# Key lookups of one pair of tiles moved to VectorE, and the norms of each pair done for both tiles together

## The chip, the cores and the metric

The kernel runs on one core of a Trainium2 chip. Its engines are TensorE (PE, matrix products), VectorE (DVE), ScalarE (ACT), GpSimd (POOL) and SyncE (SP), which only issues transfers here. The metric is the device time of one execution in microseconds.

## The reference

The kernel computes one layer for 1024 tokens of width 1024, in float32. A first sub-layer mixes tokens with a convolution module and a recurrence (RWKV-7), joins both in one output projection, and a second sub-layer retrieves single-neuron experts by product keys (PEER). Each sub-layer ends in a residual sum and a LayerNorm. What the change touches is the seam between the two:

```python
y1 = jnp.concatenate([y_conv, y_rw], axis=-1) @ w_out
x = layer_norm(ALPHA * x + gate1[:, None, :] * y1, ln1_g, ln1_b)

h2 = adaln(x, shift2, scale2)                       # a second LayerNorm
q = (h2 @ peer_wq).reshape(bsz, seq, PEER_HEADS, PEER_QDIM)
s1, s2 = ...                                        # scores against 128 keys per head and half
v1, i1 = lax.top_k(s1, PEER_TOPK)                   # 16 best of each half
v2, i2 = lax.top_k(s2, PEER_TOPK)
cand = (v1[..., :, None] + v2[..., None, :])        # 16 x 16 sums
sc, ci = lax.top_k(cand.reshape(...), PEER_TOPK)    # 16 best of these
experts = (jnp.take_along_axis(i1, ci // PEER_TOPK, axis=-1) * PEER_NKEYS
           + jnp.take_along_axis(i2, ci % PEER_TOPK, axis=-1))
gates = jax.nn.softmax(sc, axis=-1)
```

The two `take_along_axis` are the key lookups: for each of the 16 chosen candidates of a head, which key of the first half and which of the second it came from. Then each token's 128 experts give `gelu(h2 . u) * gate`, and the sum of their rows of `peer_v` is y2.

## The kernel before, in words

The 1024 tokens are eight tiles of 128; tiles go in pairs (0 and 1, 2 and 3, 4 and 5, 6 and 7). The kernel has three stages. In the first, the input projections of both halves are made. In the second, a loop over 16 chunks of 64 tokens carries the recurrence, and other work is strewn between its small products. In the third, the dense stage (lines 1222 to 1296), the activations of tiles 0 to 4 against all 16384 experts are computed on TensorE and weighted with a gate matrix, while tiles 5, 6 and 7 fetch the rows of their own experts from memory (`gather`, line 1137).

Three generators make the work between the stages, one pair at a time. `front` (line 776) makes the output projection, eight groups of products against `w_out`, brings the result back to rows by transposes (line 813), adds it to x (814), normalises, applies g1 and b1 (817 on VectorE, 818 on GpSimd), stores x1 (819), and normalises again for the second sub-layer; for a tile that will gather it also stores the modulated rows h2 (824 to 826). `query` (831) brings the normalised tiles to channels (`to_channels`, 217), makes sixteen projections against `wq` (line 858), whose weights come by `load_split` (167, three buffers), then the scores (866) and the 16 best of each (`best16`, 768). For tiles 6 and 7 the scores are only stored, and chosen from in the dense stage (`choose_late`, 880). For the others `choose` (892) finds the candidates and does the lookups: for each half of the key and each group of four heads, it compares a ramp with the chosen position (943, VectorE), multiplies with the indices (946, on the engine `E` that the caller names), and sums over sixteen places, on GpSimd in three halving sums and a last one (952, 954), on VectorE in one reduction (949). The caller names GpSimd for tiles 0 to 5 (878), and VectorE for tiles 6 and 7 (890).

When `choose` of a tile of the dense stage has ended, its `gate_matrix` (970) turns the chosen keys into the 128 x 128 gate of each token, four tokens at a time: comparisons on VectorE (1003, 1007), a multiply on GpSimd (1009), ScalarE for every fourth token (1012, 1013), a product on TensorE (1015), a copy into a stage buffer (1016) and one store of 2 MB for each 32 tokens (1023). The gate matrix of tile 4 is the last; its last block goes to the dense stage in SBUF (`gfirst`).

The last pair's `front`, then `query` of tiles 4 and 5, then `query` of tiles 6 and 7 stand in one list, `side`, and are stepped one after the other (line 1077); the lookups stand in the list `slow`, one step for every second step of `side`; the gates in the list `gates`, one step for every twelfth, at raised priority. The program order so written is the priority by which a planner, with its own estimate of durations, sets the order on each engine. On the chip each engine then runs its instructions in that order. Buffers are handed out by pools: `mm` has three PSUM banks, `page` 31 pages of SBUF, and `page2`, which the last pair's `front` and the lookups of tiles 4 and 5 use, 12 pages of 512 values.

Of the kernel before, what the change touches and what calls it, by code (L numbers as in the profile page):

```python
# [21 lines left out]
S = 1024  # L22
# [4 lines left out]
NH = 8  # L27
# [13 lines left out]
PB = 256  # L41
# [17 lines left out]
GPRI = 500  # L59
P2C = 1  # L60
NP2 = 12
PIN = 3
STEPS = 4, 3
RATES = 1.0, 1.0
# [19 lines left out]
def layer_kernel(ctx, tc, x, cols, c_row, cond_w, w_in, w2a2, g2, w_out, ln_rows, wq, keys, peer_u, peer_ut, peer_v, peer_vt, out):  # L84
    nc = tc.nc
    V, A, G, T = nc.vector, nc.scalar, nc.gpsimd, nc.tensor
# [10 lines left out]
    def col(n, i=None):  # L97
        a, b = COFF[n]
        return colt[:, a:b] if i is None else colt[:, a + i:a + i + 1]
# [53 lines left out]
    def mm(w=512):  # L153
        return psum.tile([128, 512], F32, tag="mm", name="mm")[:, :w]
# [4 lines left out]
    def page(name, dt=F32, w=512):  # L159
        return pgp.tile([128, max(w, 512)], dt, tag="pg", name=name)[:, :w]  # L160
# [49 lines left out]
    def normalize(dst, src):  # L210
        m, r = stats(src)
        b = small.tile([128, 1], F32, name="nbias")
        V.scalar_tensor_tensor(b, m, -1.0, r, op0=OP.mult, op1=OP.mult)
        for d_, s_ in zip(dst, src):
            A.activation(d_, s_, AF.Identity, bias=b, scale=r)
# [34 lines left out]
    def cond_some(js, pool=fe):  # L250

        for j in js:
            w = pool.tile([128, D], F32, tag="wraw", name="cw", bufs=WRAW if pool is fe else CBUF)
            ld(w, cond_w[j])
            with behind(0) if PIN & 2 else nullcontext():
                V.scalar_tensor_tensor(w, w, 1.0, silc, op0=OP.mult, op1=OP.mult, accum_out=mod[:, j:j + 1])
# [16 lines left out]
    def load_x(t, pg_):  # L273
        parts = [pg_("xt") for _ in range(2)]
        for i in range(2):
            ld(parts[i], x[128 * t:128 * t + 128, 512 * i:512 * i + 512])
        return parts
# [172 lines left out]
    slow, gates, gb, conv_left, psg, selbank = [], [], [], [], [], [None]  # L450
    ready = {}

    def behind(h):
        return tc.issue_after(ready[h].ins) if h in ready else nullcontext()
    PE_TAPS = 13

    def conv(h):
        acc = []
        for ct in range(4):
# [4 lines left out]
            acc.append(a)  # L464
            with behind(0) if PIN & 1 else nullcontext():
                V.tensor_scalar(a, win(0), wk(0), col("conv_b", ct), op0=OP.mult, op1=OP.add)
# [92 lines left out]
    for l in range(6):  # L559
# [6 lines left out]
        nm = rc.tile([128, 64], F32, name=f"offm{l}", bufs=1)  # L566
# [31 lines left out]
    kept, ys, late, normed, page2, st3, blocks = {}, {}, [], {}, [], [], [0]  # L598
# [164 lines left out]
    def duo(name, dt=F32, pg_=page):  # L763

        ps = [pg_(name, dt).rearrange("p (a t) -> p a t", a=2) for _ in range(KD // 2)]
        return ps, [ps[k // 2][:, k % 2, :] for k in range(KD)]
# [9 lines left out]
    def front(t0, pg_):  # L776

        n, nt, tile0 = PB, PB // 128, t0 // 128
        fetch = [tile0 + t in GT for t in range(nt)]
        hp, hi = duo("ychi", F32R, pg_)  # L780
        lp, lo = duo("yclo", F32R, pg_)
        for i in range(KD // 2):
            f = pg_("ycf").rearrange("p (a t) -> p a t", a=2)
            if i < 2:
                c = t0 % HALF
                ld(f, conv_d[t0 // HALF][2 * i:2 * i + 2, :, c:c + n].rearrange("g p t -> p g t"))
            else:
                for t in range(nt):
                    ld(f[:, :, 128 * t:128 * t + 128],
                       rwkv_d[tile0 + t][2 * i - 4:2 * i - 2].rearrange("g p t -> p g t"))  # L790
            A.activation(hp[i], f, AF.Copy)
            G.tensor_sub(lp[i], f, hp[i].bitcast(F32))
        yield
        y1 = duo("y1", F32, pg_)[1]
        for j in range(KD):
            w = load_split(w_out, j)
            pt = mm(n)
            yield from proj(w, (hi, lo), pt)
            A.activation(y1[j], pt, AF.Copy, scale=mod[:, 16 + j:17 + j])
        rows = {}  # L800
        for nm, src in (("g1", ln_rows[0]), ("b1", ln_rows[1])) + (
                (("sh2", mod_d[3]), ("sc2", mod_d[4])) if any(fetch) else ()):
            rows[nm] = [pg_("row_" + nm) for _ in range(2)]
            s_ = src.rearrange("a b -> (a b)") if len(src.shape) == 2 else src
            for i in range(2):
                ld(rows[nm][i], s_[512 * i:512 * i + 512][None, :].to_broadcast([128, 512]))
        xn = []
        for t in range(nt):
            xt = load_x(tile0 + t, pg_)
            for i in range(2):  # L810
                pt = mm()
                for k in range(4):
                    T.transpose(pt[:, 128 * k:128 * k + 128], y1[4 * i + k][:, 128 * t:128 * t + 128], ident)
                V.scalar_tensor_tensor(xt[i], xt[i], ALPHA, pt, op0=OP.mult, op1=OP.add)
            normalize(xt, xt)
            for i in range(2):
                V.tensor_mul(xt[i], xt[i], rows["g1"][i])
                G.tensor_add(xt[i], xt[i], rows["b1"][i])
                ld(x1_d[tile0 + t][:, 512 * i:512 * i + 512], xt[i])
            xs = [pg_("xn2") for _ in range(2)]  # L820
            normalize(xs, xt)
            if fetch[t]:
                for i in range(2):
                    V.scalar_tensor_tensor(xt[i], rows["sc2"][i], 1.0, xs[i], op0=OP.add, op1=OP.mult)
                    G.tensor_add(xt[i], xt[i], rows["sh2"][i])
                    ld(h2_d[tile0 + t][:, 512 * i:512 * i + 512], xt[i])
            xn.append(xs)
            yield
        normed[t0] = xn

    def query(t0):

        n, nt, tile0 = PB, PB // 128, t0 // 128
        fetch = [tile0 + t in GT for t in range(nt)]
        xn = normed.pop(t0)
        hi, lo = duo("h2hi", F32R)[1], duo("h2lo", F32R)[1]

        def keep(k, h, l):
            for w, f in enumerate((h, l)):
                for t in range(nt):  # L840
                    if not fetch[t]:
                        d = 128 * DT.index(tile0 + t)
                        ld(h2t_d[w, k, :, d:d + 128], f[:, 128 * t:128 * t + 128].bitcast(F32))

        to_channels(xn, lambda k: mod[:, 24 + k:25 + k], lambda k: modp[:, k, 1:2], hi, lo, keep)
        yield
        vi = [page("vi").rearrange("p (q h a r) -> p q h a r", q=2, h=NH, a=2) for t in range(nt)
              if tile0 + t not in score_d]
        val = [t[:, 0] for t in vi]
        idx = [t[:, 1].bitcast(U32) for t in vi]  # L850
        for g in range(4):
            kt = pgp.tile([128, 4, 128], F32, tag="pg", name="keys")
            ld(kt, keys[:, 4 * g:4 * g + 4, :])
            qt = []
            for m in range(4):
                w = load_split(wq, 4 * g + m)
                pt = mm(n)
                yield from proj(w, (hi, lo), pt)
                if m % 2 == 0:
                    qp = page("qt").rearrange("p (a t) -> p a t", a=2)  # L860
                A.activation(qp[:, m % 2, :], pt, AF.Copy)
                qt.append(qp[:, m % 2, :])
            for t in range(nt):
                ps = mm()
                for m in range(4):
                    T.matmul(ps[:, 128 * m:128 * m + 128], qt[m][:, 128 * t:128 * t + 128], kt[:, m, :],
                             start=True, stop=True)
                s = page("s12")
                A.activation(s, ps, AF.Copy)
                if tile0 + t in score_d:  # L870
                    ld(score_d[tile0 + t][g], s)
                    yield
                    continue
                for m in range(4):
                    best16(val[t][:, 2 * g + m // 2, m % 2], idx[t][:, 2 * g + m // 2, m % 2], s[:, 128 * m:128 * m + 128])
                    yield
        for t in range(len(vi)):
            slow.append(choose(tile0 + t, val[t], idx[t], 0, NH, 4, lambda nm, d, w, p=page2[0] if t0 == S - 2 * PB and P2C else page: p(nm, d, w), G))

    def choose_late(tt, lt):  # L880

# [191 lines left out]
    st3.append(pg2x.enter_context(tc.tile_pool(name="st3", bufs=1, side="right")))  # L1073
    pg2 = pg2x.enter_context(tc.tile_pool(name="pg2", bufs=NP2, side="right"))
    page2.append(lambda name, dt=F32, w=512: pg2.tile([128, max(w, 512)], dt, tag="pg2", name=name)[:, :w])
# [146 lines left out]
    for g in range(32):  # L1222
# [4 lines left out]
        for e in range(4):  # L1227
# [7 lines left out]
            for bs in NBLK:  # L1235
                p = md(NW) if g == 0 and e < 3 and bs.start else mg(NW)
                i = 0
# [12 lines left out]
        if g == 31:  # L1250
            xts = []
# [9 lines left out]
        for half in range(2):  # L1261
# [3 lines left out]
            for t in range(NT):  # L1265
# [3 lines left out]
                p = md()  # L1269
# [17 lines left out]
                if g == 31 and half == 1:  # L1287

                    xt = xts[t]
# [53 lines left out]
```

## Time and profile before

| | |
|---|---|
| time, median of 3 runs | 3232.09 us (3221.16 to 3239.63) |
| the profiled execution's own time | 3249.06 us |
| its span, first to last instruction | 3247.3 us |
| mean granted TensorE clock | 0.950 |
| busy: PE, DVE, POOL, ACT | 94%, 78%, 56%, 37% |
| moved from and to memory | 921.86 MB, 284 GB/s on average |

Durations in the profile are those of one execution, which took 17 us longer than the median of the runs. Line numbers are those of the kernel before. A line that belongs to a helper, as 215 in `normalize`, stands for all its callers. In a row of the timeline the columns are start, length, engine, line, operation, and in brackets the idle time of the engine before it and what ended it.

### The profile page before, as it was taken

To read this page: it belongs to the slowest core of one execution; us is meant where nothing else is said; L and a number is where in the kernel's file an instruction comes from. 1 tells how busy PE (TensorE), PEld (TensorE's weight loads), DVE (VectorE), ACT (ScalarE), POOL (GpSimd) and SP (SyncE) were. 2 spreads that over 40 slices of the span, in tenths; PEclk is the share of its full clock that TensorE was granted. 3 is DMA by queue.
4 is the path that set the end of the run, shared out by engine and by line. 5 is a ranking of instruction groups with operands and counts; after the bars stand their busy time and mean duration, and the time that the engine had idled before them with its cause. 6 is when DMAs were issued, how large, how long until landed. Compare 5 with 4: busy or idle time off the path is not lost.

```text
span 3247.3 us, 54840 instructions
## 1 busy us (share of the span) xinstructions
PE 3038.9 (94%) x20400; PEld 2638.9 (81%) x20400; DVE 2527.4 (78%) x5588; ACT 1202.3 (37%) x2343; POOL 1824.3 (56%) x1448
## 2 busy tenths in 40 slices
PE   6968999999899689899999999999999999999995
PEld 4735667588788689889898898888989899999994
DVE  6379565756978889759899999887878777778778
ACT  5562453343344486463223232322323232222322
POOL 2410112133442853567777677677777777787872
PEclk8979998969889899999999999999999999999997
DMA  8876464268556899899998889899999999999994
GB/s 305 291 209 228 144 190 145 99 194 309 178 194 205 278 282 332 300 317 342 332 337 311 327 304 327 292 323 352 329 352 327 350 331 349 330 346 329 343 339 183
DMA packets 411500, 921.86 MB, mean 284 GB/s; under 512 B 81712, under 2 KB 221536, under 8 KB 389216
## 3 DMA queue, kind: packets, MB, share of 16 engines
q1 hardware_dynamic: 218400, 473.71, 42.2%
q0 software_dynamic: 110592, 402.70, 34.0%
q10 hardware_dynamic: 82240, 41.94, 4.6%
q8 instruction: 160, 2.62, 0.3%
q14 instruction: 108, 0.88, 0.1%
HBM read 788.38 MB, written 129.85 MB: 283 GB/s over the span
## 4 chain that ended last, share of the span: by engine, by line
PE 45%; DVE 10%; DMA 4%; issue 3%; POOL 1%; ACT 1%; ACTq 0%; POOLq 0%; DVEq 0%
PE mg L1240 22%; PE md L1274 20%; DVE gy L1173 1%; PE mm L189 1%; DMA grow<-peer_v,eid 1%; DVE yacc L1279 1%; DVE grow L1166 1%; PE mgate L1015 1%; DMA wsplit<-split_wq 1%; DMA grow<-peer_u,eid 1%; POOL grow L1158 1%; DMA G_d<-stage 0%; DVE ob L1007 0%; DVE oa L1003 0%; DVE ltkg L949 0%
## 5 line engine op out<-in xcount | busy, mean ns | idle before, releaser
L1240 PE MATMUL mg<-h2h,uhi 128*128 128x320 f32 x2024 | 628.9, 311 | 10.4 <-DVE al L1246 10.3
L1240 PE MATMUL mg<-h2l,uhi 128*128 128x320 f32 x2024 | 627.6, 310 | 0.0
L1240 PE MATMUL mg<-h2h,ulo 128*128 128x320 f32 x2024 | 626.7, 310 | 0.0
L1173 DVE SCALAR_TENSOR_TENSOR gy<-grow,gz,gy 128x1024 f32<-128x1024 f32 x381 | 487.7, 1280 | 16.6 <-DMA grow<-peer_v,eid 14.6
L1274 PE MATMUL md<-vhi,ah 128*128 128x512 f32 x1280 | 492.5, 391 | 7.0 <-ACT ah L1245 5.6
L1274 PE MATMUL md<-vhi,al 128*128 128x512 f32 x1280 | 498.1, 390 | 0.7 <-DVE al L1246 0.7
L1274 PE MATMUL md<-vlo,ah 128*128 128x512 f32 x1280 | 496.4, 390 | 0.0
L1166 DVE SCALAR_TENSOR_TENSOR grow<-grow,gh 128x1024 f32<-128x1024 f32 x384 | 460.6, 1210 | 31.4 <-DMA grow<-peer_u,eid 30.7
L1158 POOL DMA_INDIRECT grow<-peer_v,eid x384 | 362.7, 944 | 197.1 <-DVE gy L1173 106.8
L1158 POOL DMA_INDIRECT grow<-peer_u,eid x384 | 362.9, 945 | 188.8 <-DVE grow L1166 87.0
L1240 PEld LDWEIGHTS mg<-h2h,uhi 128*128 128x128 f32 x2024 | 382.2, 189 | 19.9 <-DVE al L1246 14.4
L1240 PEld LDWEIGHTS mg<-h2l,uhi 128*128 128x128 f32 x2024 | 382.3, 189 | 5.2
L1240 PEld LDWEIGHTS mg<-h2h,ulo 128*128 128x128 f32 x2024 | 382.1, 189 | 2.9
L1201 POOL TENSOR_TENSOR vlo<-vraw,vhi 128x1024 fp32r<-128x1024 f32 x128 | 309.2, 2416 | 35.7 <-ACT vhi L1199 32.5
L1201 POOL TENSOR_TENSOR ulo<-uraw,uhi 128x1024 fp32r<-128x1024 f32 x128 | 309.3, 2417 | 25.1 <-ACT uhi L1199 23.3
L1279 DVE TENSOR_TENSOR yacc<-md,yacc 128x512 f32<-128x512 f32 x310 | 211.1, 685 | 134.0 <-PE md L1274 133.1
L1274 PEld LDWEIGHTS md<-vhi,ah 128*128 128x128 f32 x1280 | 239.6, 188 | 55.6 <-ACT ah L1245 8.0
L1274 PEld LDWEIGHTS md<-vlo,ah 128*128 128x128 f32 x1280 | 240.3, 188 | 49.0
L1274 PEld LDWEIGHTS md<-vhi,al 128*128 128x128 f32 x1280 | 240.3, 188 | 45.7 <-DVE al L1246 1.1
L1199 ACT ACTIVATE vhi<-vraw 128x1024 fp32r<-128x1024 f32 x128 | 135.0, 1055 | 375.6 <-DMA vraw<-peer_vt 357.5
L1009 POOL TENSOR_TENSOR ob<-ob,selt 128x384 f32<-128x384 f32 x160 | 140.3, 878 | 204.2 <-DVE ob L1007 143.3
L177 POOL TENSOR_TENSOR wsplit<-wraw,wsplit 128x1024 fp32r<-128x1024 f32 x46 | 112.8, 2454 | 240.8 <-ACT wsplit L176 228.7
(404 smaller groups left out, 6082.5 us busy)
## 6 DMA issues: line engine op xcount, KB each, us to landing
uraw<-peer_ut SPq DMA_DIRECT2D x128, 512.0 KB, 6.6
vraw<-peer_vt SPq DMA_DIRECT2D x128, 512.0 KB, 5.3
wsplit<-split_wq SPq DMA_DIRECT2D x48, 1024.0 KB, 7.3
G_d<-stage ACTq DMA_DIRECT2D x20, 2048.0 KB, 16.7
gmat<-G_d SPq DMA_DIRECT2D x32, 1024.0 KB, 8.4
cw<-cond_w SPq DMA_DIRECT2D x48, 512.0 KB, 5.0
wsplit<-split_w_out SPq DMA_DIRECT2D x24, 1024.0 KB, 7.2
split_w_in<-wsplit SPq DMA_DIRECT2D x22, 1024.0 KB, 5.4
```

The costliest lines, as they stand in the source:

```text
L177: G.tensor_sub(lo, raw, hi.bitcast(F32))
L189: T.matmul(pt, l[:, k, :], r[k], start=i == 0, stop=i == 3 * KD - 1)
L1009: G.tensor_mul(ob[:, :3], ob[:, :3], gt[:, ts.start:ts.start + 3, None].to_broadcast([128, 3, 128]))
L1015: T.matmul(pt[:, t, :], ob[:, t, :], oa[:, t, :], start=True, stop=True)
L1158: G.indirect_dma_start(out=r, out_offset=None, in_=peer_u if k < 128 else peer_v, in_offset=bass.IndirectOffsetOnAxis(ap=eid[:, k % 128:k ...
L1166: V.scalar_tensor_tensor(r, r, 1.0, ht, op0=OP.mult, op1=OP.mult, accum_out=z[:, i:i + 1])
L1173: V.scalar_tensor_tensor(y, r, z[:, i - 128:i - 127], y, op0=OP.mult, op1=OP.add)
L1199: A.activation(hi, raw, AF.Copy)
L1201: G.tensor_sub(lo, raw, hi.bitcast(F32))
L1240: T.matmul(p, l[:, k, :], r[k][:, bs], start=i == 0, stop=i == 3 * KD - 1)
L1274: T.matmul(p, l[:, ts], r[:, e % 2, :], start=e == 0 and q == 0, stop=e == 3 and q == 2)
L1279: ins = V.tensor_add(ya, p, ya)
```

## The change

Two things change. In `query`, the engine that `choose` is given becomes VectorE where the pair begins at token 512 or later. That is the pair of tiles 4 and 5 alone, since the next pair goes by `choose_late`. In `front`, for all four pairs, both x tiles are loaded at once; the residual sums of both tiles come first, then the first normalisation of both, then g1 and b1 for both, then the second normalisation of both, and only then, in program order, the stores of x1 and of h2. The pages of the normalised tiles are asked for together, after g1 and b1. The generator pauses four times instead of twice.

```diff
+LV = 512
@@ front
-        xn = []
-        for t in range(nt):
-            xt = load_x(tile0 + t, pg_)
+        xts = [load_x(tile0 + t, pg_) for t in range(nt)]
+        for t, xt in enumerate(xts):
             for i in range(2):
                 pt = mm()
                 for k in range(4):
                     T.transpose(pt[:, 128 * k:128 * k + 128], y1[4 * i + k][:, 128 * t:128 * t + 128], ident)
                 V.scalar_tensor_tensor(xt[i], xt[i], ALPHA, pt, op0=OP.mult, op1=OP.add)
+        yield
+        for xt in xts:
             normalize(xt, xt)
+        yield
+        for t, xt in enumerate(xts):
             for i in range(2):
                 V.tensor_mul(xt[i], xt[i], rows["g1"][i])
                 G.tensor_add(xt[i], xt[i], rows["b1"][i])
+        yield
+        xn = [[pg_("xn2") for _ in range(2)] for _ in range(nt)]
+        for xs, xt in zip(xn, xts):
+            normalize(xs, xt)
+        for t, xt in enumerate(xts):
+            for i in range(2):
                 ld(x1_d[tile0 + t][:, 512 * i:512 * i + 512], xt[i])
-            xs = [pg_("xn2") for _ in range(2)]
-            normalize(xs, xt)
+        yield
+        for t in range(nt):
             if fetch[t]:
+                xt, xs = xts[t], xn[t]
                 for i in range(2):
                     V.scalar_tensor_tensor(xt[i], rows["sc2"][i], 1.0, xs[i], op0=OP.add, op1=OP.mult)
                     G.tensor_add(xt[i], xt[i], rows["sh2"][i])
                     ld(h2_d[tile0 + t][:, 512 * i:512 * i + 512], xt[i])
-            xn.append(xs)
-            yield
         normed[t0] = xn
@@ query
-            slow.append(choose(..., G))
+            slow.append(choose(..., V if t0 >= LV else G))
```

More of the change, by code (lines that the diff above doesn't have):

```diff
@@ L877, in query @@
         for t in range(len(vi)):
-            slow.append(choose(tile0 + t, val[t], idx[t], 0, NH, 4, lambda nm, d, w, p=page2[0] if t0 == S - 2 * PB and P2C else page: p(nm, d, w), G))
+            slow.append(choose(tile0 + t, val[t], idx[t], 0, NH, 4, lambda nm, d, w, p=page2[0] if t0 == S - 2 * PB and P2C else page: p(nm, d, w), V if t0 >= LV else G))
     def choose_late(tt, lt):
```

## The prediction

> **What bounds the kernel now.** First the page, for the engines' shares; then the busy time by stretch, to find where TensorE is not full; then the chain that ended last; then single instructions around the changed lines.
>
> The page's first lines say that TensorE is busy 94% of the span:
>
> ```profile
> span 3247.3 us, 54840 instructions
> PE 3038.9 (94%) x20400; PEld 2638.9 (81%) x20400; DVE 2527.4 (78%) x5588; ACT 1202.3 (37%) x2343; POOL 1824.3 (56%) x1448
> ```
>
> By stretch (start:end, length, busy us of PE, PEld, DVE, ACT, POOL with counts, granted clock, DMA share, GB/s):
>
> ```profile
> 600.00:1020.00 420.00, 398.69 (x4335) 341.59 (x4335) 302.23 (x1063) 181.55 (x403) 148.57 (x121) 0.85 0.60 202
> 1100.00:1140.00 40.00, 27.55 (x182) 25.97 (x181) 27.62 (x49) 20.17 (x44) 32.67 (x43) 0.83 0.74 244
> 1160.00:1180.00 20.00, 14.31 (x115) 13.21 (x113) 12.09 (x22) 12.13 (x32) 9.93 (x12) 0.99 1.05 352
> 1180.00:1240.00 60.00, 54.25 (x395) 49.43 (x396) 50.36 (x102) 51.42 (x130) 33.18 (x36) 0.95 0.90 263
> 1240.00:1300.00 60.00, 58.83 (x501) 58.11 (x499) 59.61 (x295) 36.08 (x84) 21.62 (x24) 1.00 0.96 339
> 1300.00:1360.00 60.00, 49.55 (x360) 47.27 (x360) 44.33 (x217) 18.02 (x47) 36.42 (x37) 0.91 0.80 272
> 1360.00:1385.00 25.00, 25.00 (x217) 24.79 (x215) 15.55 (x29) 18.11 (x45) 12.88 (x19) 1.00 1.04 375
> 1385.00:1420.00 35.00, 32.09 (x240) 30.43 (x240) 19.38 (x35) 28.17 (x67) 18.21 (x20) 1.00 0.86 266
> 1420.00:3185.00 1765.00, 1746.85 (x9781) 1591.18 (x9780) 1468.03 (x2588) 500.97 (x824) 1336.96 (x1022) 1.00 0.92 332
> ```
>
> From 1420 us on, in the dense expert stage, TensorE is busy 1746.85 of 1765 us at full clock. Nothing the change touches lies there, so that stage keeps its length and only its start can move. The start is set before 1420 us, and what can be won is TensorE idle time there: 12.45 us in 1100:1140, 5.69 in 1160:1180, 5.75 in 1180:1240, 1.17 in 1240:1300, 10.45 in 1300:1360, none in 1360:1385, 2.91 in 1385:1420: 38.4 us together. The chain of waits over the last of these (start, us, what):
>
> ```profile
> 1223.36 6.09 DMA h_d<-xt
> 1229.46 4.92 DMA xt<-x
> ...
> 1314.32 4.84 DMA wsplit<-split_wq
> 1319.29 4.61 PE mm L189 x24
> ...
> 1328.58 7.63 DMA wsplit<-split_wq
> 1336.35 4.60 PE mm L189 x24
> ...
> 1342.74 2.88 PE mm L189 x24
> 1345.64 8.89 DMA wsplit<-split_wq
> ...
> 1392.32 15.54 DMA G_d<-stage
> ...
> 1414.38 7.33 PE mg L1240 x50
> ```
>
> The query projection of the last pair (tiles 6 and 7) goes from weight load to weight load, and after a wait the same 24 products take 4.61 us instead of 2.88 (4.61 and 4.60 after the first two waits shown, 2.88 behind other work). From 1414.38 us on the chain is the dense stage's. There is no TensorE work to put into the holes, because the only other work left, the gate matrix of tile 4, has not begun: its first comparison on VectorE stands at 1358.63 us after 14.11 us of idling, for a copy of tile 4's selection.
>
> ```profile
> 1301.10 0.34 DVE L907 TENSOR_TENSOR cand<-vi 128x64 f32<-128x64 f32 x2
> 1319.17 2.49 DVE L943 TENSOR_TENSOR oh<-iota_q,tkb 128x1024 bf16<-128x1024 bf16 x4
> 1321.58 2.42 DVE L907 TENSOR_TENSOR cand<-vi 128x128 f32<-128x128 f32 x4
> 1324.86 2.96 DVE L907 TENSOR_TENSOR cand<-vi 128x128 f32<-128x128 f32 x2
> 1358.63 0.69 DVE L1003 TENSOR_TENSOR oa<-iota,selbank 128x512 f32<-128x512 f32 x1 [14.11 <-ACT selneg L993]
> 1319.99 9.62 POOL L946 TENSOR_TENSOR oh<-oh,tkb 128x1024 bf16<-128x1024 bf16 x4 [19.64 <-issue]
> 1361.62 0.58 POOL L954 TENSOR_TENSOR tkg<-oh 128x64 f32<-128x64 bf16 x2
> ```
>
> The lookups of tiles 4 and 5 hold GpSimd from 1319.99 to 1362.20 us, 42 us, and tile 4's selection waits for them. While GpSimd does so, VectorE is slow too: two candidate sums take 2.96 us at 1324.86, where two of half that width took 0.34 us at 1301.10.
>
> **The lookups on VectorE.** Which durations does VectorE need? Tiles 6 and 7 already look up there, at half the width:
>
> ```profile
> L946 DVE TENSOR_TENSOR loh<-loh,ltkb x16: 673/678/3471, 1552.7 to 2169.0; 128x512 bf16<-128x512 bf16 x16
> L949 DVE TENSOR_REDUCE ltkg<-loh x16: 1106/1148/1181, 1559.8 to 2195.8; 128x32 f32<-128x512 bf16 x16
> L943 DVE TENSOR_TENSOR oh<-iota_q,tkb x24: 676/683/2406, 834.6 to 1343.6; 128x1024 bf16<-128x1024 bf16 x24
> L943 DVE TENSOR_TENSOR loh<-iota_q,ltkb x16: 409/419/2748, 1551.8 to 2165.4; 128x512 bf16<-128x512 bf16 x16
> ```
>
> The comparison costs 419 ns at 512 elements and 683 at 1024, so 155 ns is fixed. With that, a multiply of 1024 elements costs 155 + 2 x 523 = 1.20 us and a reduction 155 + 2 x 993 = 2.14 us: estimates from these rows. A tile has four such blocks, 13.4 us, and two tiles 26.7 us. They replace the multiply, three halving sums and last sum per block on GpSimd, 42 us as they ran. Tile 4's comparisons begin at 1319.17 and end 2.49 us later; with 13.4 us behind them its selection is there at 1335 us and its gate matrix begins near 1337 instead of 1358.6, 21 us sooner. From the earlier start, TensorE fills the holes of 1300:1360, and the last of its gate products leave 1385:1420. Upper bound: both idle sums, 13.4 us, and some 5 us more, if each of the three projections behind a wait ran at 2.88 rather than 4.61 us; lower bound none, if VectorE is the next to be late. VectorE has 15.67 + 9.45 us free in 1300:1385 and gets back about 4 us of the 2.42 + 2.96 us of slow candidate sums (six of them, which at the 0.17 us of 1301.10, twice for their width, are some 1.5 us), for 26.7 us more: it is just enough, and only because tile 5's lookup is needed by nothing before the gathers of the dense stage. What is late next is the gate's own stores: a stage buffer is free again only 15.54 us after its store went out. The DMA share of 0.80 in 1300:1360 leaves room; 1.04 in 1360:1385 does not. I take 10 us.
>
> [...]
>
> **The two tiles abreast.** Each pair's x tiles were loaded one after the other. The second load stood on SyncE's queue behind the first tile's x1 stores (and h2 stores), and for the pair 6, 7 it also waited for the first tile's buffer, by the chain above:
>
> ```profile
> 1097.85 1.57 SPq L276 DMA_DIRECT2D xt<-x  x2
> 1124.96 0.42 SPq L276 DMA_DIRECT2D xt<-x  x1
> 1181.88 1.57 SPq L276 DMA_DIRECT2D xt<-x  x2
> 1229.46 1.18 SPq L276 DMA_DIRECT2D xt<-x  x2
> 1131.83 0.68 DVE L814 SCALAR_TENSOR_TENSOR xt<-xt,mm 128x512 f32<-128x512 f32 x1
> 1234.47 0.69 DVE L814 SCALAR_TENSOR_TENSOR xt<-xt,mm 128x512 f32<-128x512 f32 x1 [1.63 <-DMA xt<-x]
> 1190.26 0.60 PE L813 MATMUL mm<-ident,y 128*128 128x128 f32 x4
> ```
>
> The first tiles' loads were issued at 1097.85 and 1181.88 us, the second tiles' at 1124.96 and 1229.46. This costs more than the tile's own delay. The transposes (L813) of the second tile are done by 1190.9 us, and their two PSUM banks of the three in the pool are held until the residual sums of 1234.47 us read them. For 44 us the query projections of tiles 4 and 5 have one bank. The same happens for pair 4, 5 until 1131.83 us, while the output projection of the last pair runs.
>
> Pair 6, 7: its pool has 12 pages; eight hold the four rows, and the first x tile gets the two that the first transposes free. The second gets its two after the last transposes, at about 1191 us; with the load's 4.92 us and its issue the sums come near 1197 instead of 1234 us. The four pages of the normalised tiles must then wait until both tiles have used g1 and b1, which puts them near 1220 us, where the first one was before. The new load passes four stores on SyncE; these are only read later. Of the 11.4 us idle in 1160:1240 the first half (1160:1180) stays, since the first x load, at 1181.88, is issued no sooner. I take 4 us; bounds 0 and 11.4.
>
> Pair 4, 5: the x tiles come together, both banks are free some 24 us sooner. In 1100:1140 TensorE has 12.45 us idle, but GpSimd is busy 32.67 of 40 there with the lookups of tiles 2 and 3, which stay, and most of that idle time goes with them. I take 4 us; bounds 0 and 12.45.
>
> Pairs 0, 1 and 2, 3 lie inside the recurrence (600:1020, 21.3 us idle of 420). The same instructions are issued, in another order, beside a chain of small products. I take 0: TensorE work of the recurrence covers it; a bound of 5 us each way, a quarter of that idle time. The h2 multiply (L824) now follows closely on the x1 store it must wait for; one such wait, up to a landing of about 6 us as in the chain's h2 store, would hold VectorE's gate comparisons behind it. I take 0, since the second normalisation still lies between, and keep 6 us for the range. The added yields only spread the same instructions; nothing.
>
> **Sum.** 10 + 4 + 4 = 18 us. The profiled execution took 3249.06 us, so 3231 us for one like it; that execution lies 17 us above the median of 3232.09, so the prediction is 3214 us.
>
> **Rivals.** *Nothing to speak of.* The chain of 1305 to 1358 us runs through weight loads and not through the lookups. If the gate stores, moved into that stretch, slow the weight loads as much as the filled holes save, there remain the 2.9 us of 1385:1420 and some of the fronts: 3226 to 3230 us. For it: DMA at 1.04 in 1360:1385. Against it: 0.80 in 1300:1360.
>
> *Slower, by VectorE.* It is at 59.61 of 60 us in 1240:1300 already. If its order puts both lookups, 26.7 us, ahead of tile 4's gate comparisons, these begin after 1358.6 us, and every one of the 32 groups then shares VectorE with what is left. With 4 us returned this is 23 us more: 3255 us. It decides if the first comparison of tile 4 comes later than 1358.6 us. Against it: the gates have a raised priority, and tile 4 stands before tile 5. [...]
>
> *All of the idle time.* If the query of pair 4, 5 starts sooner as well, and fills 1100:1240, up to 38.4 us go: 3194 us, about 3204 if three quarters (29 us) of it go.
>
> *The pages don't allow it.* If the second x tile of pair 6, 7 still waits for a page, the 4 us of that pair are lost, and the normalised tiles come later: 3218 to 3222 us.
>
> **Numbers.** About 0.5%, 16 us, can be told from no change in this kernel. The forecast 0.45 (its own range 3204 to 3224; two thirds beyond 16 us), all idle time 0.15 (faster), nothing 0.17, pages 0.08 (both same), slower 0.15. Faster 0.45, same 0.40, slower 0.15. The range runs from 3192, near the upper bound of the gain, to 3246, which leaves out most of the slower case.
>
> **What would show it.** Right: the lookups (L946, L949) as VectorE instructions of about 1.2 and 2.1 us; first gate comparison of tile 4 near 1337 us less what the fronts bring; gate products between 1337 and 1360 us; the second x load of the last pair before 1200 us and its L814 sums with it; last gate product some 18 us before 1414; the dense stage as long as before. Wrong: TensorE as idle as now before the dense stage, later stores of G_d, or a dense stage that is longer.

## The result and the profile after

The changed kernel took 3254.09 us (median of 17 runs, 3242.73 to 3260.17), the kernel before, on the same chip, 3232.48 us (median of 17 runs, 3221.16 to 3250.56). The ratio is 1.0064, 95% interval 1.0049 to 1.0078: slower by 0.64%, where 0.56% faster (3214 us) was forecast. The profiled execution took 3253.09 us, close to its median, so unlike the one of before it is a typical one.

The page of the changed kernel, engines' shares. VectorE has 22.4 us more to do than before, GpSimd 33.5 us less, TensorE about the same.

```profile
span 3251.3 us, 54811 instructions
PE 3030.7 (93%) x20400; PEld 2634.9 (81%) x20400; DVE 2549.8 (78%) x5604; ACT 1200.3 (37%) x2342; POOL 1790.8 (55%) x1408
```

The changed kernel by the same stretches as in the prediction (start:end, length, busy us of PE, PEld, DVE, ACT, POOL with counts, granted clock, DMA share, GB/s):

```profile
600.00:1020.00 420.00, 387.98 (x4268) 334.10 (x4266) 304.03 (x1084) 178.85 (x400) 149.74 (x121) 0.87 0.60 205
1100.00:1140.00 40.00, 29.18 (x169) 26.55 (x168) 37.09 (x66) 25.13 (x53) 34.14 (x39) 0.76 0.56 181
1160.00:1180.00 20.00, 20.00 (x176) 20.00 (x176) 12.97 (x24) 16.30 (x41) 9.08 (x11) 1.00 1.09 359
1180.00:1240.00 60.00, 50.77 (x371) 46.42 (x371) 54.38 (x118) 50.32 (x128) 35.89 (x39) 0.94 0.94 293
1240.00:1300.00 60.00, 58.15 (x493) 57.39 (x492) 55.07 (x270) 33.89 (x81) 18.84 (x21) 1.00 0.96 324
1300.00:1360.00 60.00, 53.15 (x406) 51.21 (x405) 55.04 (x242) 29.44 (x73) 8.09 (x9) 0.91 0.78 279
1360.00:1385.00 25.00, 22.71 (x193) 22.30 (x192) 24.63 (x33) 12.30 (x30) 13.65 (x9) 1.00 0.88 290
1385.00:1420.00 35.00, 29.36 (x234) 28.57 (x233) 18.45 (x34) 25.25 (x60) 16.56 (x19) 0.95 1.04 352
1420.00:3185.00 1765.00, 1747.11 (x9795) 1591.98 (x9794) 1461.67 (x2585) 501.08 (x825) 1335.47 (x1020) 1.00 0.93 332
```

Three readings. The dense stage is as busy as before (1747.11 us of 1765 against 1746.85), so the loss lies ahead of it. In 1300:1360 the lookups did what was meant: GpSimd falls from 36.42 to 8.09 us, and TensorE has 3.6 us less idle time; but 1360:1385 and 1385:1420 together lose 5.0 us. And the recurrence, 600:1020, where a loss of nothing was forecast, has 10.7 us more idle TensorE time.

The lookups as VectorE instructions, in the timeline of the changed kernel (start, length, engine, line, operation; L955 and L958 are L946 and L949 of before, L1012 is L1003):

```profile
1329.74 4.62 DVE L955 TENSOR_TENSOR oh<-oh,tkb 128x1024 bf16<-128x1024 bf16 x4
1334.83 8.03 DVE L958 TENSOR_REDUCE tkg<-oh 128x64 f32<-128x1024 bf16 x4
1347.35 0.66 DVE L1012 TENSOR_TENSOR oa<-iota,selbank 128x512 f32<-128x512 f32 x1
...
1365.26 2.35 DVE L955 TENSOR_TENSOR oh<-oh,tkb 128x1024 bf16<-128x1024 bf16 x2
1367.53 0.67 DVE L1012 TENSOR_TENSOR oa<-iota,selbank 128x512 f32<-128x512 f32 x1
1368.59 2.35 DVE L955 TENSOR_TENSOR oh<-oh,tkb 128x1024 bf16<-128x1024 bf16 x2
1370.86 0.67 DVE L1012 TENSOR_TENSOR oa<-iota,selbank 128x512 f32<-128x512 f32 x1
1371.92 4.11 DVE L958 TENSOR_REDUCE tkg<-oh 128x64 f32<-128x1024 bf16 x2
1375.94 0.68 DVE L1012 TENSOR_TENSOR oa<-iota,selbank 128x512 f32<-128x512 f32 x1
```

A multiply takes 1.16 us and a reduction 2.01 us; 1.20 and 2.14 were estimated. Tile 4's first gate comparison comes at 1347.35 us, 11.3 us sooner than before. But tile 5's lookup is cut into the row of tile 4's comparisons, which from 1363 to 1381 us come only every 3 to 5 us. The last gate product and, behind it, the first dense product into the `mg` banks come at 1420.5 us, 6 us later than in the profile of before.

The last pair's second x tile, same timeline; before, these rows stood at 1229.46 and 1234.47 us:

```profile
1202.79 1.14 SPq L277 DMA_DIRECT2D xt<-x  x2
1212.52 0.69 DVE L814 SCALAR_TENSOR_TENSOR xt<-xt,mm 128x512 f32<-128x512 f32 x1
```

So both edits do locally what they say. What they cost is found when the time ahead of the dense stage is cut at three events that every kernel has: the seventh of the recurrence's sixteen state updates (L708, in the changed kernel L709), the sixteenth, and the first dense product that goes to the `mg` banks (L1240, L1249; products of the same line that go to `md` banks start 18 to 33 us before it). "Nine steps" is from the first to the second, "seam" from the second to the third, "rest" from the third to the end of the span. The two windows of the kernel before:

```profile
664.20:1024.70 360.50, 343.59 (x3818) 305.19 (x3817) 266.82 (x1026) 153.65 (x346) 132.22 (x113) 0.84 0.64 216
1024.70:1414.10 389.40, 328.13 (x2542) 312.01 (x2542) 313.14 (x1069) 231.29 (x553) 221.64 (x233) 0.93 0.86 287
```

and of the changed kernel:

```profile
659.50:1034.20 374.70, 343.72 (x3877) 305.65 (x3875) 269.79 (x1057) 155.08 (x351) 134.30 (x115) 0.86 0.64 217
1034.20:1420.50 386.30, 327.38 (x2490) 313.13 (x2491) 332.11 (x1054) 228.49 (x547) 185.86 (x192) 0.91 0.85 282
```

The nine steps are 14.2 us longer with the same busy TensorE time (343.72 us against 343.59): it is idle for 31.0 us instead of 16.9. The seam is 386.3 us against 389.4: of the forecast 18 us, 3 at most arrived there.

### The profile page after: what moved, and what is told of

It is laid out like the page before. It is cut to its first block, busy times and chain, and to the rows that moved or that the text cites. A ratio compares the mean times of both kernels' runs of the same rounds, so it can differ in the third digit from the quotient of the medians.

```text
span 3251.3 us, 54811 instructions
## 1 busy us (share of the span) xinstructions
PE 3030.7 (93%) x20400; PEld 2634.9 (81%) x20400; DVE 2549.8 (78%) x5604; ACT 1200.3 (37%) x2342; POOL 1790.8 (55%) x1408
## 4 chain that ended last, share of the span: by engine, by line
PE 44%; DVE 10%; DMA 3%; issue 3%; POOL 1%; ACT 1%; SPq 0%; ACTq 0%; POOLq 0%; DVEq 0%
PE mg L1249 21%; PE md L1283 20%; DVE grow L1175 2%; DVE gy L1182 2%; PE mm L190 2%; DMA grow<-peer_v,eid 1%; DVE yacc L1288 1%; PE mgate L1024 1%; DMA G_d<-stage 1%; DMA grow<-peer_u,eid 0%; POOL vlo L1210 0%; DVE mg L1253 0%; DVE ltkg L958 0%; POOL grow L1167 0%; DMA vraw<-peer_vt 0%
## 5 line engine op out<-in xcount | busy, mean ns | idle before, releaser
L1249 PE MATMUL mg<-h2h,uhi 128*128 128x320 f32 x2024 | 628.4, 310 | 12.9 <-DVE al L1255 12.9
L1249 PE MATMUL mg<-h2l,uhi 128*128 128x320 f32 x2024 | 626.9, 310 | 0.0
L1249 PE MATMUL mg<-h2h,ulo 128*128 128x320 f32 x2024 | 626.5, 310 | 0.0
L1249 PEld LDWEIGHTS mg<-h2h,uhi 128*128 128x128 f32 x2024 | 381.6, 189 | 22.5 <-DVE al L1255 17.3
L1249 PEld LDWEIGHTS mg<-h2l,uhi 128*128 128x128 f32 x2024 | 381.7, 189 | 4.7
L1249 PEld LDWEIGHTS mg<-h2h,ulo 128*128 128x128 f32 x2024 | 381.5, 189 | 3.2
L1210 POOL TENSOR_TENSOR vlo<-vraw,vhi 128x1024 fp32r<-128x1024 f32 x128 | 309.1, 2416 | 29.6 <-ACT vhi L1208 27.3
```

The lines of the kernel that those rows point to most:

```text
L1210: G.tensor_sub(lo, raw, hi.bitcast(F32))
L1249: T.matmul(p, l[:, k, :], r[k][:, bs], start=i == 0, stop=i == 3 * KD - 1)
```

## The experiments

The same cuts for all kernels, each from its own two windows. "Idle" is TensorE's idle time in steps and seam together; ratio and interval are of the timed runs against the kernel before on the same chip, the four stages are of one profile each.

| kernel | what it has | steps | seam | idle | rest | ratio (95%) |
|---|---|---|---|---|---|---|
| before | | 360.5 | 389.4 | 78.2 | 1833.2 | |
| b2 | the same again | 360.6 | 385.7 | 76.0 | 1828.0 | 1.0006 (0.9987 to 1.0025) |
| after | both edits | 374.7 | 386.3 | 89.9 | 1830.8 | 1.0064 (1.0049 to 1.0078) |
| e1 | lookups on VectorE only | 351.9 | 392.4 | 90.6 | 1837.3 | 1.0044 (1.0022 to 1.0066) |
| e2 | fronts abreast only | 374.5 | 384.3 | 88.1 | 1824.9 | 1.0068 (1.0043 to 1.0093) |
| e3 | fronts of pairs 0,1 and 2,3 only | 371.6 | 399.5 | 101.8 | 1831.4 | 1.0109 (1.0081 to 1.0136) |
| e4 | lookups, fronts of 4,5 and 6,7 | 352.4 | 395.6 | 91.0 | 1839.9 | 1.0074 (1.0045 to 1.0104) |
| e5 | tile 4's lookup only | 361.6 | 390.8 | 86.3 | 1846.8 | 1.0067 (1.0038 to 1.0096) |
| e6 | one pause more per tile | 350.8 | 394.0 | 84.3 | 1833.0 | 1.0033 (1.0012 to 1.0055) |
| e7 | fronts of 4,5 and 6,7 only | 356.6 | 397.8 | 83.7 | 1825.6 | 1.0043 (1.0022 to 1.0065) |
| e8 | front of 6,7 only | 351.1 | 392.5 | 82.7 | 1828.5 | 1.0005 (0.9984 to 1.0027) |
| e9 | front of 4,5 only | 360.5 | 388.6 | 79.4 | 1833.8 | 1.0017 (0.9994 to 1.0040) |
| e10 | both x loads at once only | 375.1 | 388.1 | 100.1 | 1831.2 | 1.0049 (1.0029 to 1.0069) |
| e11 | lookups, front of 6,7 | 362.3 | 388.8 | 84.1 | 1845.0 | 1.0036 (1.0016 to 1.0057) |
| e12 | after, early queries held back | 350.6 | 403.5 | 89.6 | 1843.7 | 1.0095 (1.0064 to 1.0126) |
| e13 | e2, early queries held back | 354.6 | 410.8 | 87.1 | 1827.6 | 1.0044 (1.0021 to 1.0066) |
| e14 | before, early queries held back | 366.4 | 393.8 | 91.6 | 1826.0 | 1.0040 (1.0019 to 1.0060) |

### Which edit costs

Four kernels with a part of the change each. e1 sets the engine of the lookups and leaves `front` as it was (with the engine goes the number of pauses: two in each block on VectorE, five on GpSimd, so e1 too changes how the generators interleave); e2 has the new `front` and the lookups on GpSimd; e3 and e4 take the new `front` for some pairs only:

```diff
 e1: +LV = 512   ...   V if t0 >= LV else G
 e3: +if t0 < 512:   new front   +else:   old front      (no LV)
 e4: +if t0 >= 512:  new front   +else:   old front      (with LV)
```

(In short form; "new front" and "old front" stand for the lines of the change.)

> Only the lookups of tiles 4 and 5 go to VectorE; front is as before. Changed kernel: 1.0064 of before. Theory A (the loss comes from the fronts inside the recurrence): 0.994 to 1.000, first gate comparison of tile 4 near 1340 us less the recurrence's delay. Theory B (VectorE: tile 5's lookup stands between tile 4's gate groups and stretches them from 57 to 77 us): 1.002 to 1.006, and the same stretch here. Theory C (any change of the program order makes the planner lay the seam out anew, with no tie to one edit): anything, and not adding up with the next run.

> Only the fronts go abreast, for all pairs; the lookups stay on GpSimd. Theory A: 1.003 to 1.008, recurrence ends about 10 us later than in the kernel before. Theory B: 0.995 to 1.001. Theory C: no sum with the run of the lookups alone.

> Abreast only for pairs 0, 1 and 2, 3, inside the recurrence; pairs 4, 5 and 6, 7 and the lookups as before. Theory A: 1.003 to 1.008, the recurrence ends 5 to 10 us later. Theory B: 0.998 to 1.002.

> The lookups on VectorE, and abreast for pairs 4, 5 and 6, 7 only; pairs 0 to 3 as before. Theory A: 0.993 to 0.999, recurrence as before until the front of pair 4, 5. Theory B: 1.002 to 1.006, tile 4's gate matrix still some 77 us long.

Each of the four is slower than the kernel before, by 0.44, 0.68, 1.09 and 0.74%. The parts do not add up: the lookups (0.44) and the fronts (0.68) together cost 0.64, and two of the four fronts (1.09, six runs) cost more than all four, though these two intervals just overlap. So no single edit is the culprit; what adds up is read from the stages. The nine steps are 371.6 to 374.7 us in the three kernels that have pairs 0,1 and 2,3 abreast (after, e2, e3), and 351 to 362 us in the kernels whose `front` and `query` of these pairs are as before: theory A (the loss comes from the fronts inside the recurrence) holds for that stage. e4, without these fronts, should then have been fast, and was not: its seam and its rest are 6 and 7 us longer than before's.

The kernel before once more (b2), two controls, and the fronts of the last two pairs alone (the edit of e5 is shown against e1, that of e6 against the kernel before):

```diff
 e5: -V if t0 >= LV else G
     +V if t0 >= LV and t == 0 else G
 e6:                  V.scalar_tensor_tensor(xt[i], xt[i], ALPHA, pt, ...)
     +            yield
                  normalize(xt, xt)
 e7: e4 without LV
```

> The kernel before once more, unchanged, as a control of the measurement: ratio 1.000 with an interval that holds 1. Its profile gives a second look at the kernel before, whose first profiled execution (3249.06 us) lay 17 us above the median that the prediction was given. Theories A and C: the second profile keeps the recurrence's long step positions (no front burst in step 8) and a recurrence end within 5 us of 1024.7, so the first profile was typical. Rival D (the first profile was of an execution with a lower granted clock): the recurrence of this one ends near 1010 us and the gate matrix of tile 4 is ready near 1400 us, not 1414 us, and the total is 3225 to 3230 us.

> Only tile 4's lookup is on VectorE; tile 5's stays on GpSimd and the fronts stay as before. Theory B (the loss is tile 5's lookup standing between tile 4's gate comparisons on VectorE): tile 4's gate matrix starts sooner (selection transposed near 1318 to 1340 us instead of 1352) and is not stretched, so the time is 5 to 15 us under the run with both lookups on VectorE (ratio 1.0044) and at or under the kernel before: 0.997 to 1.000. Theory C (any change of the program's order costs, whichever it is): 1.003 to 1.010, like the other runs.

> The kernel before with one more hand-over point in the front, between the residual sum and the normalization of each tile: no operation is added, removed or moved to another engine, only the places where the interleaved generators take turns shift by one. Theory C: slower by 0.3 to 1 % although no work changed. Theories A and B (the loss belongs to the x loads and stores, or to the lookups): 0.998 to 1.002.

> Both tiles abreast for the pairs 4,5 and 6,7 only, no lookup on VectorE, pairs 0,1 and 2,3 as before: this is the part of the change that the prediction priced at a gain of 4 + 4 us. By the prediction's sum: ratio 0.9975 (8 us of 3230). Theory A (the loss comes from the two fronts inside the recurrence, which stay as before here): 0.996 to 0.999. Theory C: 1.003 to 1.010. Second tile's x load of the last pair near 1200 us instead of 1230 us in both.

b2 gives 1.0006, and its profile (3237.55 us) shows the same stages as the first one, to 4 us in the seam and 5 in the rest: the first profile, though 17 us above the median, showed the kernel before rightly. e5 takes away what theory B blames, and is no faster than e1 (0.67 against 0.44%, intervals overlapping): tile 5's lookup between the gate comparisons is seen in the trace, but taking it away won nothing. e6 moves no work at all, and costs 0.33%. That is theory C: a new order alone can cost some tenths of a per cent. (It need not: e8 and e9 below are new orders too.)

### The last two pairs

e8 and e9 take the new `front` for one pair alone (`if t0 == S - PB`, `if t0 == 512`).

> Both tiles abreast in the front of the last pair (6,7) alone; all else as before, so the recurrence keeps its order. Theory by stages (the price of each stage follows from its order on the engines and is the same in every run): from the end of the last pair's output projection to the first scores of tile 4, 79 us before and 68 us where pairs 4,5 and 6,7 are abreast, this pair alone brings most of it, 68 to 72 us; the recurrence's last nine steps take 351 to 361 us as before; what is won there is lost again by the fourth group of scores (76 us instead of 56 us in the run with pairs 4,5 and 6,7 abreast). Total 1.000 to 1.005. The prediction's own sum for this part: 0.9988.

> Both tiles abreast in the front of pair 4,5 alone. The dense stage keeps the order of before, instruction by instruction, so its length stays at 1792 to 1797 us. Theory by stages: the step from the output projection to tile 4's first scores stays near 79 us, if the gain there belongs to pair 6,7; the nine steps of the recurrence stay at 351 to 361 us; total 0.998 to 1.003. Theory C (any change of order costs): 1.003 to 1.010. The prediction's own sum for this part: 0.9988.

The prediction put 4 us on each of these fronts, to be won between the last output projection and the scores of tile 4. The scores of two tiles come in four groups of products. The two windows below go from the end of that projection to the end of the first group of tiles 4 and 5, and from there to the end of their fourth; first the kernel before:

```profile
1161.70:1240.50 78.80, 67.36 (x501) 61.44 (x500) 61.99 (x123) 62.88 (x158) 42.19 (x47) 0.96 0.93 283
1240.50:1296.60 56.10, 54.93 (x467) 54.34 (x466) 55.71 (x281) 32.18 (x75) 19.40 (x22) 1.00 0.96 337
```

The same two windows of e7, both fronts abreast:

```profile
1149.60:1219.00 69.40, 60.37 (x454) 55.72 (x453) 61.10 (x127) 58.19 (x146) 38.20 (x42) 0.95 0.90 286
1219.00:1295.80 76.80, 68.33 (x547) 67.34 (x545) 61.61 (x282) 40.37 (x97) 26.50 (x29) 0.93 0.89 293
```

The first window of e8, the front of pair 6,7 alone:

```profile
1148.00:1227.60 79.60, 67.79 (x499) 62.87 (x498) 70.06 (x140) 65.13 (x162) 46.03 (x50) 0.91 0.91 286
```

Both fronts together win 9.4 us in the first window, near the forecast 8 (the changed kernel: 68.0 us); the last pair's front alone wins nothing (79.6, where 68 to 72 us were expected), and pair 4,5's alone 2.9 (75.9 us in e9). In e7 the next window gives it back: 76.8 us instead of 56.1, with 80 more TensorE records in it, 78 of them gate products (208 of L1047, where before has 130 of L1015; the window ahead has 304 of them instead of 352), and 8.5 us idle instead of 1.2, of which one wait for a `wq` load takes 5.7:

```profile
PE mm L189 <- DMA wsplit<-split_wq: 5.7, 1, 5.7
```

So the query was brought forward, and gate products, 48 of which had stood ahead of the first scores, came to stand inside it. The changed kernel doesn't show this (59.6 us in that window), nor does e2 (57.6); in both the early fronts are abreast too. Why the two differ there from e7 is open.

### What the early x loads do to the recurrence

e10 has only the two loads together:

```diff
+        xts = [load_x(tile0 + t, pg_) for t in range(nt)]
         for t in range(nt):
-            xt = load_x(tile0 + t, pg_)
+            xt = xts[t]
```

> Only the two x loads of every pair stand together, ahead of the loop; residual sums, normalisations, stores and pauses stay tile after tile. Theory A (the abreast order of the sums and normalisations is what lengthens the recurrence): its nine steps stay at 351 to 361 us and the total is 0.998 to 1.002. Rival: the early loads do it (both x tiles there at once, so all transposes of a pair are made in one burst between the recurrence's products): nine steps of 370 to 375 us, total 1.004 to 1.010.

> The lookups on VectorE together with the abreast front of the last pair (6,7) alone: the whole change without what lies inside the recurrence. Theory A, simple form (only the recurrence's fronts cost, the rest of the change gains as predicted): 0.994 to 0.998. Theory by stages (the lookups win 4 us ahead of the dense stage and lose 5 to 8 us in it; the front's 11 us go again in tile 4's and 5's query): 1.002 to 1.007.

e10 has the nine steps of the changed kernel (375.1 us) and costs 0.49%: the rival of that pair of theories holds, the loads do it and not the abreast order of the sums. The two windows of the section above are 68.6 and 78.6 us in e10, like those of e7: there, too, the early loads alone do it. e11, the lookups and the front of the last pair alone, should have been a gain by the simple form of theory A; it costs 0.36%, with 362.3 us for the steps and 12 to 17 us more in the rest. The trace shows what the loads do. Timeline of the kernel before: the second tile's residual sums (L814), two state updates (L708), and the first product of the query of pair 0,1 (L189):

```profile
682.71 0.41 DVE L708 TENSOR_TENSOR SN<-SN,wc 128x256 f32<-128x256 f32 x1
694.57 0.68 DVE L814 SCALAR_TENSOR_TENSOR xt<-xt,mm 128x512 f32<-128x512 f32 x1
712.30 0.43 DVE L708 TENSOR_TENSOR SN<-SN,wc 128x256 f32<-128x256 f32 x1
721.09 0.58 PE L189 MATMUL mm<-h2hi,wsplit 128*128 128x256 f32 x1
```

The same four events of the changed kernel:

```profile
672.14 0.64 DVE L814 SCALAR_TENSOR_TENSOR xt<-xt,mm 128x512 f32<-128x512 f32 x1
675.69 0.40 DVE L709 TENSOR_TENSOR SN<-SN,wc 128x256 f32<-128x256 f32 x1
705.94 0.58 PE L190 MATMUL mm<-h2hi,wsplit 128*128 128x256 f32 x1
735.46 0.42 DVE L709 TENSOR_TENSOR SN<-SN,wc 128x256 f32<-128x256 f32 x1
```

The second tile's sums come 22 us sooner, and the first product of the query of that pair 15 us sooner (the seventh state update stands 4.7 us sooner already, so 18 and 10 us against the recurrence). Now the query's products stand ahead of the next state update instead of behind it: that step takes 59.8 us instead of 29.6. The following steps are shorter, since that work is done, but over the nine steps 14 us are lost, as waits of the recurrence's own products for VectorE; in the changed kernel

```profile
PE bank L678 <- DVE T L655: 8.8, 4, 6.7
```

is the largest (us, times, longest), and in the kernel before no such row of the nine steps is above 2.7 us.

To test this, the query of pairs 0,1 and 2,3 was held back:

```diff
     def query(t0):
...
+        for _ in range(96 if t0 < 512 else 0):
+            yield
```

> The changed kernel, with the query of the pairs 0,1 and 2,3 held back by 96 pauses at its start, so that 33 instead of 137 of its products stand between the recurrence's state update at 675.7 us and the next one. Theory A (the query's projections, let in sooner, stand ahead of the recurrence's next step): that step takes 29 to 40 us instead of 59.8, the last nine steps 355 to 365 us instead of 374.7, total 6 to 14 us under the changed kernel: ratio 1.002 to 1.005. Rival (the sums and normalisations abreast lengthen it themselves): 370 to 376 us and 1.006 to 1.008.

> As the last, without the lookups on VectorE: all fronts abreast, the query of pairs 0..3 held back. Theory A: nine steps of 355 to 365 us instead of 374.5, and with the lookups' loss gone too 0.998 to 1.003. Rival: 370 to 376 us and 1.006 to 1.009.

> The kernel before with the same hold of the query, and nothing else: what the hold costs by itself. Theory A: nine steps of 355 to 365 us as before, total 0.999 to 1.004. If the hold alone costs 10 us or more in the seam behind the recurrence, the other two runs are read by their steps and not by their totals.

Timeline of e12, the changed kernel with the query held:

```profile
678.26 0.40 DVE L709 TENSOR_TENSOR SN<-SN,wc 128x256 f32<-128x256 f32 x1
708.46 0.56 PE L190 MATMUL mm<-h2hi,wsplit 128*128 128x256 f32 x1
718.32 0.42 DVE L709 TENSOR_TENSOR SN<-SN,wc 128x256 f32<-128x256 f32 x1
```

The step takes 40.1 us, and the nine steps 350.6 us in e12 and 354.6 in e13, 20 to 24 less than without the hold. So the query's products did lengthen the recurrence. But the time did not fall as theory A expected: e12 is 0.95% slower than the kernel before (0.64% without the hold), e13 0.44% (0.68% without it, the intervals overlapping). The hold alone (e14) costs 0.40%, 5.9 us of it in the steps. The windows of e13, against 374.5 and 384.3 us without the hold (e2):

```profile
659.00:1013.60 354.60, 332.94 (x3741) 295.71 (x3740) 255.37 (x960) 151.54 (x342) 137.59 (x113) 0.83 0.63 211
1013.60:1424.40 410.80, 345.36 (x2617) 331.06 (x2617) 325.04 (x1133) 234.07 (x557) 221.30 (x233) 0.90 0.84 280
```

What the steps won, the seam lost: 18.5 us of held products (345.36 us busy against 326.84) and 8 us more idle. TensorE's idle time in both together is 87.1 us instead of 88.1, and 89.6 instead of 89.9 in e12. In these two kernels, then, a shorter recurrence brought no less idle time. That its length sets the loss is not shown by them, but not refuted either: e13 and e14 have the same hold, one with the new `front` and one with the old, and cost the same (0.44 and 0.40%), so that with the hold in place the new fronts cost nothing that can be seen, where without it they cost 0.68%. What the hold itself costs hides the answer.

### What the runs leave

Of the stages in the table, the one that goes best with the time is TensorE's idle time ahead of the dense stage. It is 76 to 78 us in the kernel before, and 79 to 102 in each of the other fifteen; the least of them (e9, 79.4; e8, 82.7) are the two that can't be told from no change, the largest (e3, 101.8) is the slowest. Over the sixteen orders it correlates with the ratio at 0.73. The changed kernel has 12.8 us more than the two profiles of before on average. A part of such a difference is of the execution and not of the order: e1, e4, e5, e7, e8, e9 and e11 have the order of before up to the end of the recurrence, and TensorE is idle for 17.0 to 23.2 us in their nine steps, against 16.9 and 17.3 in the two profiles of before. So the smallest differences in the column say nothing, and one of 12.8 us is twice that spread. The lookups on VectorE add a second term: the rest, 1824.9 to 1833.8 us without them, is 1837.3 to 1846.8 in five of the six kernels that have them, the changed kernel being the sixth (1830.8). In e1 TensorE waits longer in the first 800 us of the dense stage for a VectorE subtraction, 15.7 us against 11.1 in b2; first e1, then b2:

```profile
PE mg L1241 <- DVE al L1247: 15.7, 10, 3.1
```

```profile
PE mg L1240 <- DVE al L1246: 11.1, 9, 3.0
```

Two things stay open. Why the order of the kernel before has the least idle time is not shown; it is an observation over sixteen orders. And the idle time accounts for 13 of the 22 us. Some 8 of the other 9 go with the mean granted clock: within one kernel a run is 2.0 us longer for each 0.001 that it is lower (least squares over all timed runs, each kernel with a level of its own), and it is 0.9511 on average in the changed kernel and 0.9552 in the kernel before. Over the sixteen orders this clock, averaged over the timed runs, goes with the ratio more closely than the idle time does: the correlation is -0.86, from 0.9493 in e12 to 0.9554 in e8. That the stretch ahead of the dense stage is longer does not explain it: its mean clock is some 0.89 in the windows of before above, and 13 us more of that lower the mean of 3240 us by 0.0003 (an estimate), not by 0.0041. Whether a new order lowers the clock, or what lowers it also costs the time, was not separated. No version beat the kernel before, so none is proposed.

## Why the prediction was wrong

**Pairs 0 to 3.** The failing step is "I take 0: TensorE work of the recurrence covers it; a bound of 5 us each way". The nine steps lost 14.2 us, almost three times the bound, and e10 shows that the early loads lose them. The reasoning looked at the front's own instructions, which are the same and do fit beside the recurrence. It left out what an earlier x tile sets free: the query of the same pair, whose first product comes 15 us sooner, on the same engine. The prediction had asked that question for the seam ("what is late next") and not here.

**The lookups.** "I take 10 us": alone (e1) the lookups cost 0.44%, 14 us, where 10 were to be won. The estimates of the instructions were right (1.16 and 2.01 us), the earlier start was half right (11.3 us instead of 21, in a kernel whose recurrence ended 9.5 us later; in e1 tile 4's selection is transposed at 1318.1 us, 34 us sooner). The failing step is "From the earlier start, TensorE fills the holes of 1300:1360, and the last of its gate products leave 1385:1420". From the last scores to the dense stage e1 wins 5.6 us (25.6 instead of 31.2), but from the fourth group of scores to the eighth it loses 5.2 (91.5 instead of 86.3), and the rest is 4 to 9 us longer. That the dense stage keeps its length held for the changed kernel and failed for the lookups alone. One sum on the way is off without consequence: six candidate sums at twice 0.17 us are 2.0 us, not 1.5, so VectorE gets back 3.3 us rather than 4.

**The last two pairs.** "4 + 4" was about right in its place: 78.8 to 68.0 us. The reason given, banks held by the second tile of the last pair, fell: that pair's front alone brings the second tile's sums to 1187.79 us, 47 us sooner (33 us, counted from the end of the output projection), and leaves the window at 79.6. And the gain didn't last (e7: 0.43% slower in all, where 0.25% faster would have been the sum).

**The pauses.** "The added yields only spread the same instructions; nothing." One more pause per tile, with nothing else, costs 0.33% (e6).

**The rivals.** *Slower, by VectorE* had the sign and, by chance, the time, 3255 us; its own point of decision did not occur (first comparison of tile 4 at 1347.35 us, not after 1358.6), and e5 speaks against its mechanism. e1 agrees with this rival in sign: work moved from GpSimd to VectorE, the busier of the two in the profile of before (2527.4 us against 1824.3), cost 0.44%. The runs don't show that VectorE's larger share is the cause.

**What was behind all of it.** The sum treated each edit as a change of some durations in an order that otherwise stays. But the order is made anew from the whole program: in e1, which changes only the lookups, TensorE's products come as before up to about 1270 us (9500 of 20400 records), and from there into the dense stage, to about 2200 us, in another order. The prediction priced the local effects, in part rightly, and put nothing on the new order, in the range neither.

## What to carry to other kernels

Where a planner lays out the whole program, measure first what a change of the order alone can cost, with an edit that moves no work (here one more pause, 0.33%): an expected gain of that size can't be argued from local durations alone. When something is made ready sooner, ask on every stage what it sets free and ahead of which chain that lands; here a load brought forward put a query's products, 15 us sooner, ahead of the next step of a recurrence. And judge such a change over the whole stretch, by the bounding engine's idle time and by the timed runs, not by when one stage ends: in e12 and e13 the nine steps of the recurrence got 20 to 24 us shorter, and neither kernel was faster by more than its interval.

## What the runs showed of the hardware

The granted clock of TensorE is not the same in the same stretch of the same order. e1 and the kernel before have the same instructions in the same order up to the end of the recurrence. There, one step (from the 13th state update to the 14th) takes 38.5 us in the profile of before, 39.7 in b2 and 28.8 in e1. The stretch 910 to 949 us of e1, then of b2:

```profile
910.00:949.00 39.00, 38.67 (x415) 35.34 (x414) 28.60 (x75) 21.17 (x53) 20.41 (x22) 1.00 0.71 227
```

```profile
910.00:949.00 39.00, 39.00 (x345) 33.29 (x344) 22.27 (x38) 18.64 (x46) 14.83 (x12) 0.73 0.47 158
```

TensorE is busy throughout in both, at a clock of 1.00 and of 0.73, with 415 records against 345. Some 10 us, 0.3% of the kernel, thus come and go between executions in this one step. The other kernels with that order fall on the same two sides: 30.3 and 28.8 us in e4 and e8, at a clock of 0.97 and 1.00, and 38.3 to 39.7 us in e5, e7, e9 and e11, at 0.68 to 0.70. That is most of the spread from 351 to 362 us in the table's column of steps; the changed kernel's nine steps are 22 to 24 us longer than those of e1, e4 and e8, and 12 to 18 us longer than those of the others. Over the whole span the mean granted clock is 0.95 in these kernels (0.9493 to 0.9554, averaged over the timed runs of each). What sets the clock in such a stretch is not shown.

On VectorE the lookup's two bf16 tensor-tensor operations do not take the same time at the same width. The multiply, whose second operand is spread along the innermost axis, has a median of 1212 ns at 1024 elements (L955 of the changed kernel, eight of them; the 1.16 us above are a fourth of the row of four), where the comparison, L943 of before, has 683. At 512 elements it is 678 ns (L946 of before) against 419. Why they differ was not shown.
